# Feed-forward part of a hybrid decoder layer: one gate/up unit of the next group moved ahead of a group's down units, groups of 3, 4 and 4 slabs, transposes queued ahead of weight splits

## The chip, the cores and the metric

The kernel runs on one core of a Trainium2 chip. The metric is the device time of one execution in microseconds (us). The core has a matrix engine (TensorE, PE in the rows, with its weight loader PEld), a vector engine (VectorE, DVE), a scalar engine (ScalarE, ACT), GpSimd (POOL) and a queue engine (SyncE, SP), which here only issues DMAs. Each of them works through its own queue of instructions in order and waits on semaphores of the others.

## What is computed

One decoder layer on 256 tokens of width 2048: two attention mixers, merged and added to the input, and then a gated feed-forward part of width 5632. The change touches the last part alone:

```
hn = _rms(x, norm_ffn)                       # x: 256 x 2048, fp32
x = x + (silu(hn @ w_ffn_gate) * (hn @ w_ffn_up)) @ w_ffn_down
```

w_ffn_gate and w_ffn_up are 2048 x 5632, w_ffn_down is 5632 x 2048, all fp32 and read from HBM once.

## The kernel before, in words

**Precision.** Each product is made of three matmuls in the reduced fp32r format: an operand is split into hi (rounded, `L1059` for weights, on ACT) and lo (the rest, `L1060`, on DVE), and PE adds hi*hi, hi*lo and lo*hi (`L1084` to `L1086`) in PSUM.

**Steps and units.** The feed-forward part is a list of steps, objects of class `Pair`. A step takes two 128-row blocks of a weight (1 MB, two DMAs on SP into one of three `raw8` buffers). A plain step is 24 matmuls of 512 columns. A seven step (`mm_seven`) forms its 2x2 block product from seven instead of eight products and so needs 21 matmuls, but it has more to split: the weight is split in two parts, the second of sums that DVE forms first (`sums`, `L1051` to `L1054`). Four parts can be ahead of PE, since there are four hi/lo buffers; the sums have one.

A unit is 8 steps (or 6) that accumulate into the same PSUM banks. A gate/up unit of slab f makes 512 columns of the gated hidden activation from all of hn: steps 0, 2 and 4 are seven steps, except in slab 0, where all are plain. After the last seven step, `combine` adds the four banks of the seven-products on DVE (`L1121` to `L1124`; in the last group also the rows of the result so far, fetched by `fetch`, `L1127` to `L1130`); after the last step, `last` adds the rest (`L1141`) and `swiglu` forms the hidden slab (ACT `L1176`, DVE `L1180`) in two of the five `q2` buffers.

**Transposes.** A slab is the stationary operand of the down product, so it is transposed in two pairs by `hid_pair`: four PE transposes each (`L976`) into a PSUM bank of the kind that the seven-products use, then either `put_plain` (ACT copy `L950`, DVE difference `L951`, tile `ip`) or, for a pair that a seven step will use, `put_seven` (ACT `L958`, DVE `L962` to `L965`, ACT `L968`, DVE `L969`, tiles `F` and `i`). They hang on a step as hooks: (j, 0) before the step's matmuls, (j, 1) in the middle of them.

**Groups.** 11 slabs in groups of 4, 4 and 3. After the gate/up units of a group come its two down units (columns 0 to 1023 and 1024 to 2047 of the result), each with two steps for each slab: steps 0, 2 and 4 of 8, or 0 and 2 of 6, are seven steps. The first two groups add their result into `hacc` in HBM by accumulating DMAs on POOL; the last reads it back (`fetch`) and writes the output. Slab f is transposed in the unit that follows its gate/up unit, at the step after that unit's last seven step: step 5 of 8, step 3 of 6. For the last slab of a group this unit is the group's first down unit, whose last two steps use that slab.

**Order of instructions.** The loop at the end of the kernel goes through the steps and queues for each, in this order: `run_ffn(i)` (loads, and the splits of the parts that are now in reach), the hook (j, 0), the matmuls with the hook (j, 1) in their middle, then `combine` or `last`. On ACT and DVE the splits queued at a step thus stand ahead of its transposes.

In the text, "unit d0.0" is the first down unit of group 0, "g3" the gate/up unit of slab 3, and steps are counted from 0.

Of the kernel before, what the change touches and what calls it, by code (L numbers as in the profile page):

```python
# [14 lines left out]
P = 128  # L15
# [38 lines left out]
def hybrid_block(ctx: ExitStack, tc: tile.TileContext, x, norm_attn, w_in, fox_f_bias,  # L54
# [37 lines left out]
    def wk(shape, tag, bufs, dt=F32):  # L92
        pool = keep if tag in ("qs", "sm") else work
        return pool.tile(shape, dt, tag=tag, name=nm(tag), bufs=bufs)
# [8 lines left out]
    def load_x(q):  # L103
        for t in range(NT):
            nc.sync.dma_start(xin[t][:, q * 512:(q + 1) * 512], x[t * P:(t + 1) * P, q * 512:(q + 1) * 512])
# [7 lines left out]
    def load_vectors():  # L113
        nc.sync.dma_start(vec[16:32, :], norm_ffn.rearrange("(k p) -> k p", p=P))
        row = lambda a: a.rearrange("(o p) -> o p", o=1)
        nc.sync.dma_start(vec[32:33, :], row(fox_q_gain))
        nc.sync.dma_start(vec[33:34, :], row(fox_k_gain))
        for j, g in enumerate((nsa_q_gain, nsa_kc_gain, nsa_ks_gain, nsa_kw_gain)):
            nc.sync.dma_start(vec[34 + j:35 + j, :], row(g[0:P]))
            for o in (0, DK - P):  # L120
                nc.sync.dma_start(vec[38 + j:39 + j, o:o + DK - P], row(g[P:DK]))
        nc.sync.dma_start(pek, cmp_pe_k.rearrange("(j i) d -> j (i d)", i=2))
        nc.sync.dma_start(pev, cmp_pe_v)
        nc.sync.dma_start(fbias, fox_f_bias.partition_broadcast(P))
# [15 lines left out]
    def finish(tk):  # L140
        while not tk.over:
            tk.step()
        if tk in tasks:
            tasks.remove(tk)
# [12 lines left out]
    def load(ch):  # L157
        ch.raw = wpool.tile([P, 1024], F32, tag="raw", name=nm("raw"), bufs=RAW_BUFS)
        eng = nc.scalar if ch is stream[0] else nc.sync
        eng.dma_start(ch.raw[:, :ch.nkb * ch.n].rearrange("p (k n) -> p k n", k=ch.nkb),  # L160
                      ch.src.rearrange("(k p) n -> p k n", p=P))
        if ch is stream[0]:
            warm = wk([P, 16], "sm", 11)
            nc.scalar.activation(warm[:, 0:1], ident[:, 0:1], AF.Exp)
# [755 lines left out]
    def open2():  # L920
        left.close()
        pools[2] = left.enter_context(tc.tile_pool(name="pool2", bufs=1, reuse_waits="tile"))
# [5 lines left out]
    def p2(shape, tag, bufs, dt=F32):  # L928
        return pools[2].tile(shape, dt, tag=tag, name=nm(tag), bufs=bufs)
# [6 lines left out]
    SH = (0, 2, 4)  # L936
# [34 lines left out]
    def transpose_pair(make, srcs, c, seven, gains=None, where="tp"):  # L971

        b = bank(where)
        for k in range(2):
            for o, t in enumerate((1, 0) if seven and k == 0 else (0, 1)):
                nc.tensor.transpose(b[:, (2 * k + o) * P:(2 * k + o + 1) * P],  # L976
                                    srcs[t][:, c + k * P:c + (k + 1) * P], ident)
        dst = make(seven)
        (put_seven if seven else put_plain)(dst, b, gains)
        return dst  # L980

    hT = [None] * 8
    htask = {}
# [173 lines left out]

    hid = {}
    hsrc = {}
    GROUPS = ((0, 4), (4, 8), (8, 11))  # L1160
    SD = {8: (0, 2, 4), 6: (0, 2)}

    def make_hid(seven):
# [2 lines left out]
    def hid_pair(f, a, g):  # L1166
        f0, f1 = GROUPS[g]
        hid[f, a] = transpose_pair(make_hid, hsrc[f], a * 256, (f - f0) * 2 + a in SD[2 * (f1 - f0)],
                                   where="acc")

    def swiglu(f):
        def done(c, in_psum):
            g = {}
            for t in range(NT):
                g[t] = wk([P, 512], "qs", 4) if in_psum else c[t, 0]
                nc.scalar.activation(g[t], c[t, 0], AF.Silu, scale=rh[:, t:t + 1])  # L1176
            hsrc[f] = []
            for t in range(NT):
                o = p2([P, 512], "q2", 5) if in_psum else c[t, 1]
                nc.vector.scalar_tensor_tensor(o, c[t, 1], rh[:, t:t + 1], g[t], op0=ALU.mult, op1=ALU.mult)  # L1180
                hsrc[f].append(o)
        return done

    def two(w, r0, c0):
        return lambda kp: [w[r0 + kp * 2 * P:r0 + (kp + 1) * 2 * P, c:c + 512] for c in (c0, c0 + 512)]

    def down(g, i):
        pre = {}
        final = g == len(GROUPS) - 1
        cols = lambda c: slice((2 * i + c) * 512, (2 * i + c + 1) * 512)  # L1190

        def fetch():
            for t in range(NT):
                for c in range(2):
                    pre[t, c] = p2([P, 512], "q2", 5) if c else wk([P, 512], "qs", 4)
                    nc.gpsimd.dma_start(pre[t, c], hacc[t * P:(t + 1) * P, cols(c)])

        def done(c, in_psum):
            for t, h in ((0, 0), (1, 0), (0, 1), (1, 1)):
                rows = slice(t * P, (t + 1) * P)  # L1200
                if final:
                    nc.sync.dma_start(out[rows, cols(h)], c[t, h])
                else:
                    nc.gpsimd.dma_start(hacc[rows, cols(h)], c[t, h], accum_op=ALU.add)
        return fetch, done, (lambda: pre) if final else None

    pend = []

    def transposes(j):

        if not pend or j is None:
            return {}
        q = pend.pop()
        return {(j + 1, o): lambda o=o: hid_pair(q, o, g_of[q]) for o in range(2)}

    for g, (f0, f1) in enumerate(GROUPS):
        for f in range(f0, f1):
            sevens = SH if f else ()
            order = list(range(8))
            unit(order, sevens, lambda kp, f=f: [w[kp * 2 * P:(kp + 1) * 2 * P, f * 512:(f + 1) * 512]  # L1220
                                                 for w in (w_ffn_gate, w_ffn_up)],
                 lambda kp: hT[kp], swiglu(f), lambda kp: [htask[kp // 2]], transposes(max(sevens) if sevens else None))
            pend.append(f)
        n = 2 * (f1 - f0)
        order = list(range(n))
        for i in range(2):
            fetch, done, add = down(g, i)
            hooks = transposes(max(SD[n]))
            if add:
                hooks[0, 0] = fetch  # L1230
            unit(order, SD[n], two(w_ffn_down, f0 * 512, i * 1024),
                 lambda kp, f0=f0: hid[f0 + kp // 2, kp % 2], done, None, hooks, add)
    g_of = {f: g for g, (f0, f1) in enumerate(GROUPS) for f in range(f0, f1)}


    nload = nsplit = 0
    ffn = next(j for j, ch in enumerate(stream) if isinstance(ch, Pair))

    def split_ahead(i):
        return min(i + min(SPLIT_AHEAD, 2 + i // 4), ffn - 1)  # L1240

    def split_next():
        nonlocal nsplit
        split(stream[nsplit])
        nsplit += 1
        if nsplit == 1:
            transpose_gain(xT[0], xin, 0, VA)

    def run_att(i, ch):
        nonlocal nload  # L1250
        if i == n_att:
            open2()
        while nload < min(i + LOAD_AHEAD, ffn):
            if nload - nsplit >= RAW_BUFS:
                if nsplit <= split_ahead(i):
                    split_next()
                    continue
                break
            if nload < 8 and nload % 2 == 0:
                load_x(nload // 2)  # L1260
            load(stream[nload])
            nload += 1
            if nload == 9:
                load_vectors()
        while nsplit <= split_ahead(i):
            split_next()
# [28 lines left out]
    for i, ch in enumerate(stream):  # L1295
        if i < ffn:
            run_att(i, ch)
        if i + 8 >= ffn:
            run_ffn(i)
        if ch.need:  # L1300
            for tk in ch.need():
                finish(tk)
        if ch.pre:
            ch.pre()
        ch.mm(ch)
        if i in (0, 2, 4):
            transpose_gain(xT[i // 2 + 1], xin, i // 2 + 1, VA)
        if ch.done:
            ch.done()
        if i >= ffn:  # L1310
            ch.free()
            slot()
            slot()
            continue
        ch.raw = ch.hi = ch.lo = None
        if ch.nkb < 4:
            slot()
# [32 lines left out]
```

## Time and profile before

| | us |
|---|---|
| median of 3 runs (1457.8 to 1458.56) | 1458.3 |
| profiled execution, its own time | 1459.65 |
| span in that execution, first to last instruction | 1457.9 |
| feed-forward part in it, from 735.6 | 722 |

| engine | busy us | share of the span |
|---|---|---|
| PE | 1438.0 | 99% |
| PEld | 1206.2 | 83% |
| DVE | 1093.8 | 75% |
| ACT | 746.2 | 51% |
| POOL | 56.4 | 4% |

The profile is one execution, recorded by the hardware profiler. Times are counted from the first instruction. A row of the timeline gives start, duration, engine, line of the kernel, operation, output and inputs; a bracket at its end gives how long the engine had been idle before it and whose result ended that. A matmul of 512 columns is shown with 0.39 us, though the next one starts after 0.227 us: they overlap, and their ends are modelled. So one reads PE by starts, not by durations.

### The profile page before, as it was taken

The numbers are of one execution on the slowest core, as the hardware profiler recorded it, in microseconds if no ns is written. First come the engines' busy times: TensorE is split into PE (matmuls) and PEld (weight loads), VectorE is DVE, ScalarE is ACT, GpSimd is POOL, SyncE is SP. The second block draws the span as 40 slices with busy tenths as digits, with TensorE's granted clock in tenths as the row PEclk, the third lists the DMA queues.
The fourth block names the chain that finished last, engine by engine and source line by source line (L and its number), as shares of the span: only waits on it lengthen the run. The fifth ranks groups of instructions, "written<-read, shape, count | busy, mean of one in ns | idle before, by whom it ended". The sixth has DMA issues, their size and how long they took to land.

```text
span 1457.9 us, 18092 instructions
## 1 busy us (share of the span) xinstructions
PE 1438.0 (99%) x6772; PEld 1206.2 (83%) x6772; DVE 1093.8 (75%) x1408; ACT 746.2 (51%) x937; POOL 56.4 (4%) x75
## 2 busy tenths in 40 slices
PE   9999999999999999999999999999999999999978
PEld 7888888998888888888888888788888878888867
DVE  7766766776776555555666999878999997889976
ACT  6466554455666344445644455444554554445532
POOL 2001010000000000000000000000000000000000
PEclk9999999999999999999999999999999999999989
DMA  7576876457444666656764556678655667866653
GB/s 276 173 231 199 267 236 185 126 166 210 145 131 151 203 188 184 187 184 221 242 225 165 182 194 218 215 202 222 200 185 202 202 220 190 226 202 206 227 174 116
DMA packets 155395, 287.06 MB, mean 197 GB/s; under 512 B 9598, under 2 KB 32220, under 8 KB 155180
## 3 DMA queue, kind: packets, MB, share of 16 engines
q1 hardware_dynamic: 151260, 275.87, 59.9%
q0 software_dynamic: 3872, 9.78, 3.2%
q8 instruction: 53, 0.87, 0.2%
q10 hardware_dynamic: 176, 0.27, 0.1%
q14 instruction: 34, 0.28, 0.1%
HBM read 277.48 MB, written 8.40 MB: 196 GB/s over the span
## 4 chain that ended last, share of the span: by engine, by line
PE 96%; DVE 2%; issue 1%; ACT 0%; DMA 0%; POOL 0%; ACTq 0%; POOLq 0%; DVEq 0%
PE acc L193 14%; PE acc L194 14%; PE acc L195 14%; PE m L1086 12%; PE m L1084 12%; PE m L1085 12%; PE acc L1085 4%; PE acc L1084 4%; PE acc L1086 4%; PE m L536 1%; DVE lo L1060 1%; PE m L537 1%; PE acc L976 1%; DMA raw<-in_w_in_dram 0%; PE m L372 0%
## 5 line engine op out<-in xcount | busy, mean ns | idle before, releaser
L171 DVE TENSOR_TENSOR lo<-raw,hi 128x1024 fp32r<-128x1024 f32 (+5 forms) x261 | 306.4, 1179 | 169.8 <-ACT hi L170 169.2
L193 PE MATMUL acc<-hi,u 128*128 128x512 f32 (+4 forms) x960 | 374.8, 390 | 0.2 <-ACT u L270 0.2
L194 PE MATMUL acc<-lo,u 128*128 128x512 f32 (+4 forms) x960 | 368.3, 384 | 0.4 <-DVE lo L171 0.4
L195 PE MATMUL acc<-hi,u 128*128 128x512 f32 (+4 forms) x960 | 368.3, 384 | 0.0
L170 ACT ACTIVATE hi<-raw 128x1024 fp32r<-128x1024 f32 (+5 forms) x261 | 262.8, 1022 | 179.0 <-PE acc L195 166.3
L1060 DVE TENSOR_TENSOR lo<-raw,hi 128x2048 fp32r<-128x2048 f32 (+1 forms) x132 | 276.9, 2100 | 49.9 <-ACT hi L1059 49.8
L1059 ACT ACTIVATE hi<-raw 128x2048 fp32r<-128x2048 f32 (+1 forms) x132 | 231.9, 1762 | 142.7 <-PE m L1086 99.5
L195 PEld LDWEIGHTS acc<-hi,u 128*128 128x128 f32 x960 | 180.7, 188 | 33.1 <-DVE u L271 0.2
L193 PEld LDWEIGHTS acc<-hi,u 128*128 128x128 f32 x960 | 180.9, 188 | 30.7 <-ACT u L270 0.5
L194 PEld LDWEIGHTS acc<-lo,u 128*128 128x128 f32 x960 | 181.0, 189 | 30.2 <-DVE lo L171 1.0
L1084 PE MATMUL m<-hi,hp 128*128 128x512 f32 x400 | 157.4, 393 | 0.0
L1086 PE MATMUL m<-hi,hp 128*128 128x512 f32 x400 | 156.2, 390 | 0.0
L1085 PE MATMUL m<-lo,hp 128*128 128x512 f32 x400 | 155.9, 390 | 0.0
L1059 ACT ACTIVATE hi<-sums 128x2048 fp32r<-128x2048 f32 x46 | 88.2, 1917 | 126.2 <-DVE sums L1054 83.8
L1060 DVE TENSOR_TENSOR lo<-sums,hi 128x2048 fp32r<-128x2048 f32 x46 | 105.4, 2292 | 32.6 <-ACT hi L1059 32.6
L1086 PE MATMUL m<-hi,ip 128*128 128x512 f32 x224 | 90.1, 402 | 12.4 <-DVE ip L951 12.4
L1084 PE MATMUL m<-hi,ip 128*128 128x512 f32 x224 | 89.9, 401 | 0.0
L1085 PE MATMUL m<-lo,ip 128*128 128x512 f32 x224 | 89.4, 399 | 0.0
L1086 PEld LDWEIGHTS m<-hi,hp 128*128 128x128 f32 x400 | 75.1, 188 | 15.8
L1085 PEld LDWEIGHTS m<-lo,hp 128*128 128x128 f32 x400 | 75.2, 188 | 15.2
L1084 PEld LDWEIGHTS m<-hi,hp 128*128 128x128 f32 x400 | 75.2, 188 | 15.1
L1086 PEld LDWEIGHTS m<-hi,ip 128*128 128x128 f32 x224 | 43.5, 194 | 23.0 <-DVE ip L951 13.7
(300 smaller groups left out, 1791.2 us busy)
## 6 DMA issues: line engine op xcount, KB each, us to landing
raw<-in_w_in_dram SPq DMA_DIRECT2D x127, 512.0 KB
raw<-in_w_ffn_gate_dram SPq DMA_DIRECT2D x88, 512.0 KB
raw<-in_w_ffn_up_dram SPq DMA_DIRECT2D x88, 512.0 KB
raw<-in_w_ffn_down_dram SPq DMA_DIRECT2D x88, 512.0 KB
raw<-in_w_out_dram SPq DMA_DIRECT2D x32, 512.0 KB
raw<-in_w_in_dram SPq DMA_DIRECT2D x24, 384.0 KB
raw<-in_w_up_fox_dram SPq DMA_DIRECT2D x16, 512.0 KB
raw<-in_w_up_nsa_dram SPq DMA_DIRECT2D x16, 512.0 KB
```

The source lines that it names most:

```text
L170: nc.scalar.activation(hi[:, :m], ch.raw[:, :m], AF.Copy)
L171: nc.vector.tensor_tensor(lo[:, :m], ch.raw[:, :m], hi[:, :m].bitcast(F32), op=ALU.subtract)
L193: nc.tensor.matmul(o, h, ch.hi[:, j], start=first and j == 0, stop=False)
L194: nc.tensor.matmul(o, h, ch.lo[:, j], start=False, stop=False)
L195: nc.tensor.matmul(o, l, ch.hi[:, j], start=False, stop=last and j == w - 1)
L536: nc.tensor.matmul(o, s, ch.hi[:, j], start=j == 0, stop=False)
L537: nc.tensor.matmul(o, s, ch.lo[:, j], start=False, stop=j == 3)
L1059: nc.scalar.activation(h, src, AF.Copy)
L1060: nc.vector.tensor_tensor(l, src, h.bitcast(F32), op=ALU.subtract)
L1084: nc.tensor.matmul(o, h, hi, start=n == 0, stop=False)
L1085: nc.tensor.matmul(o, h, lo, start=False, stop=False)
L1086: nc.tensor.matmul(o, l, hi, start=False, stop=n + 1 == total[key])
```

## The change

The groups become 3, 4 and 4 slabs. The gate/up unit of the next group's first slab is put ahead of a group's two down units, so that the last slab of the first two groups is transposed in that gate/up unit (step 5), and that next slab itself in the group's second down unit (step 3 of 6 or 5 of 8). In the last group, where no slab follows, the first down unit takes its steps in the order 0, 1, 2, 4, 3, 5, 6, 7, so that its three seven steps are the places 0, 2 and 3, and the last slab is transposed at place 4. And in the loop the hook (j, 0) of a feed-forward step is called ahead of `run_ffn(i)`, so that its transposes, and the loads of `fetch`, are queued before that step's loads and weight splits; the hook (j, 1) stays where it was.

```
--- before.py
+++ after.py
@@ -1157,7 +1157,7 @@
 
     hid = {}
     hsrc = {}
-    GROUPS = ((0, 4), (4, 8), (8, 11))
+    GROUPS = ((0, 3), (3, 7), (7, 11))
     SD = {8: (0, 2, 4), 6: (0, 2)}
 
     def make_hid(seven):
@@ -1204,33 +1204,39 @@
                     nc.gpsimd.dma_start(hacc[rows, cols(h)], c[t, h], accum_op=ALU.add)
         return fetch, done, (lambda: pre) if final else None
 
-    pend = []
-
-    def transposes(j):
-
-        if not pend or j is None:
-            return {}
-        q = pend.pop()
-        return {(j + 1, o): lambda o=o: hid_pair(q, o, g_of[q]) for o in range(2)}
-
+    def transposes(f, j):
+
+        return {(j, o): lambda o=o: hid_pair(f, o, g_of[f]) for o in range(2)}
+
+    def gate_up(f, hooks):
+        sevens = SH if f else ()
+        unit(list(range(8)), sevens, lambda kp: [w[kp * 2 * P:(kp + 1) * 2 * P, f * 512:(f + 1) * 512]
+                                                 for w in (w_ffn_gate, w_ffn_up)],
+             lambda kp: hT[kp], swiglu(f), lambda kp: [htask[kp // 2]], hooks)
+
+    def down_unit(g, i, order, hooks):
+        f0, f1 = GROUPS[g]
+        fetch, done, add = down(g, i)
+        if add:
+            hooks = {**hooks, (0, 0): fetch}
+        unit(order, SD[2 * (f1 - f0)], two(w_ffn_down, f0 * 512, i * 1024),
+             lambda kp: hid[f0 + kp // 2, kp % 2], done, None, hooks, add)
+
+    g_of = {f: g for g, (f0, f1) in enumerate(GROUPS) for f in range(f0, f1)}
+    at = {8: 5, 6: 3}
     for g, (f0, f1) in enumerate(GROUPS):
-        for f in range(f0, f1):
-            sevens = SH if f else ()
-            order = list(range(8))
-            unit(order, sevens, lambda kp, f=f: [w[kp * 2 * P:(kp + 1) * 2 * P, f * 512:(f + 1) * 512]
-                                                 for w in (w_ffn_gate, w_ffn_up)],
-                 lambda kp: hT[kp], swiglu(f), lambda kp: [htask[kp // 2]], transposes(max(sevens) if sevens else None))
-            pend.append(f)
         n = 2 * (f1 - f0)
         order = list(range(n))
-        for i in range(2):
-            fetch, done, add = down(g, i)
-            hooks = transposes(max(SD[n]))
-            if add:
-                hooks[0, 0] = fetch
-            unit(order, SD[n], two(w_ffn_down, f0 * 512, i * 1024),
-                 lambda kp, f0=f0: hid[f0 + kp // 2, kp % 2], done, None, hooks, add)
-    g_of = {f: g for g, (f0, f1) in enumerate(GROUPS) for f in range(f0, f1)}
+        more = g + 1 < len(GROUPS)
+
+        for f in range(f0 + (1 if g else 0), f1 + (1 if more else 0)):
+            gate_up(f, transposes(f - 1, 5) if f > f0 + (1 if g else 0) else {})
+        if more:
+            down_unit(g, 0, order, {})
+            down_unit(g, 1, order, transposes(f1, at[n]))
+        else:
+            down_unit(g, 0, [0, 1, 2, 4, 3, 5, 6, 7], transposes(f1 - 1, 4))
+            down_unit(g, 1, order, {})
 
 
     nload = nsplit = 0
@@ -1295,12 +1301,14 @@
     for i, ch in enumerate(stream):
         if i < ffn:
             run_att(i, ch)
+        if i >= ffn and ch.pre:
+            ch.pre()
         if i + 8 >= ffn:
             run_ffn(i)
         if ch.need:
             for tk in ch.need():
                 finish(tk)
-        if ch.pre:
+        if i < ffn and ch.pre:
             ch.pre()
         ch.mm(ch)
         if i in (0, 2, 4):
```

## Rows read from the trace of the kernel before

**Rows 1.** The page, first part: busy time, share of the span, instructions.

```profile
PE 1438.0 (99%) x6772; PEld 1206.2 (83%) x6772; DVE 1093.8 (75%) x1408; ACT 746.2 (51%) x937; POOL 56.4 (4%) x75
```

**Rows 2.** Waits of PE and PEld: total us, times, longest us.

```profile
PE m L1086 <- DVE ip L951: 12.4, 3, 7.5
...
PEld acc L1085 <- DVE lo L1060: 1.9, 8, 0.5
```

**Rows 3.** Timeline, PE: first matmuls of steps of d0.0 and d0.1, d1.0, d2.0.

```profile
939.25 0.39 PE L1084 MATMUL m<-hi,ip 128*128 128x512 f32 x1
...
949.09 0.39 PE L1084 MATMUL m<-hi,ip 128*128 128x512 f32 x1
...
954.53 0.39 PE L1084 MATMUL acc<-hi,i 128*128 128x512 f32 x1
...
1196.97 0.39 PE L1084 MATMUL m<-hi,ip 128*128 128x512 f32 x1
...
1206.57 0.39 PE L1084 MATMUL m<-hi,ip 128*128 128x512 f32 x1
...
1401.41 0.39 PE L1084 MATMUL m<-hi,ip 128*128 128x512 f32 x1
...
1417.07 0.39 PE L1084 MATMUL m<-hi,ip 128*128 128x512 f32 x1
```

**Rows 4.** Timeline, PE: the three matmuls that waited for a transposed slab.

```profile
942.33 0.50 PE L1086 MATMUL m<-hi,ip 128*128 128x512 f32 x1 [2.47 <-DVE ip L951]
...
1200.05 0.80 PE L1086 MATMUL m<-hi,ip 128*128 128x512 f32 x1 [2.46 <-DVE ip L951]
...
1409.54 0.80 PE L1086 MATMUL m<-hi,ip 128*128 128x512 f32 x1 [7.52 <-DVE ip L951]
```

**Rows 5.** Stages: us, each engine's busy time, granted clock, DMA share, GB/s.

```profile
960.00:1000.00 40.00, 40.00 (x178) 33.15 (x177) 34.12 (x29) 18.94 (x12) 3.46 (x4) 1.00 0.81 234
1000.00:1150.00 150.00, 149.96 (x671) 123.71 (x670) 135.16 (x117) 80.28 (x56) 0.00 (x0) 1.00 0.65 204
1395.00:1425.00 30.00, 22.48 (x92) 18.14 (x91) 20.86 (x23) 9.69 (x7) 2.16 (x4) 0.83 0.59 187
```

**Rows 6.** Timeline, DVE and one row of ACT: step 5 of g3; step 2 of d0.0.

```profile
892.59 2.28 DVE L1060 TENSOR_TENSOR lo<-raw,hi 128x2048 fp32r<-128x2048 f32 x1
894.79 1.22 DVE L1051 TENSOR_TENSOR sums<-raw 128x1024 f32<-128x1024 f32 x1
...
897.38 1.75 DVE L1060 TENSOR_TENSOR lo<-raw,hi 128x1536 fp32r<-128x1536 f32 x1
899.05 0.29 DVE L962 TENSOR_TENSOR F<-F 128x128 f32<-128x128 f32 x1
...
901.14 1.09 DVE L969 TENSOR_TENSOR i<-F,i 128x896 fp32r<-128x896 f32 x1 [1.08 <-ACT i L968]
901.50 1.91 ACT L1059 ACTIVATE hi<-sums 128x2048 fp32r<-128x2048 f32 x1
902.15 0.68 DVE L951 TENSOR_TENSOR ip<-acc,ip 128x512 fp32r<-128x512 f32 x1
903.44 2.29 DVE L1060 TENSOR_TENSOR lo<-sums,hi 128x2048 fp32r<-128x2048 f32 x1 [0.60 <-ACT hi L1059]
...
916.28 2.29 DVE L1060 TENSOR_TENSOR lo<-sums,hi 128x2048 fp32r<-128x2048 f32 x1 [0.38 <-ACT hi L1059]
```

**Rows 7.** Timeline, PEld and DVE: step 2 and step 5 of d0.0.

```profile
918.63 0.19 PEld L1085 LDWEIGHTS acc<-lo,i 128*128 128x128 f32 x1 [0.20 <-DVE lo L1060]
...
941.59 1.28 DVE L951 TENSOR_TENSOR ip<-acc,ip 128x512 fp32r<-128x512 f32 x2
```

**Rows 8.** Timeline of d2.0: PE's step 2, and DVE around it.

```profile
1390.15 0.39 PE L1084 MATMUL acc<-hi,i 128*128 128x512 f32 x1
...
1390.87 4.49 DVE L1060 TENSOR_TENSOR lo<-raw,hi 128x2048 fp32r<-128x2048 f32 x2
...
1398.73 0.69 DVE L1123 TENSOR_TENSOR q<-acc,qs 128x512 f32<-128x512 f32 x1 [2.04 <-PE acc L976]
```

## The prediction

> **What bounds the kernel.** I read the first part of the page first [rows 1]: PE is busy 99% of the span, the other engines far less. So only time in which PE stands or runs slowly can be won, unless it gets less work, and it does not: the diff only reorders. In groups of 4, 4 and 3 the down units have 2 x (3 + 3 + 2) = 16 seven steps, in 3, 4 and 4 just as many; matmuls, transposes, splits, loads and the accumulating DMAs keep their number. Next I read the waits of PE [rows 2]: of all its waits in the feed-forward part, one matters, 12.4 us in 3 waits for the DVE half of a transposed slab (L951). The timeline places them [rows 4]: 2.47, 2.46 and 7.52 us, in the first down unit of each group, where the unit's last steps use the slab that was only just made.
>
> The wait is not all that is lost. The step beginning at 939.25 ends at 949.09 and takes 9.84 us; the next, also 24 matmuls, ends at 954.53 and takes 5.44 us [rows 3]. The stages show why [rows 5]: the granted clock, 1.00 between 960 and 1150 us, is 0.83 in the stage of the longest wait, so after it matmuls run for a while at 1.2 instead of 2.4 GHz. Reading the reader should take along: a step's length from start to start holds both losses.
>
> Why is the slab late? DVE. At step 5 its queue holds a split, sums and a second split ahead of the transposes' DVE work: in the like step of g3 that is 892.59 to 899.05, 6.5 us [rows 6]; in d0.0 L951 comes only at 941.59, 2.3 us after PE wanted it at the step begun at 939.25 [rows 3, 7]. And DVE has little room: 135.16 of 150 us busy [rows 5].
>
> **What the change removes.** Three long steps, each against 5.44 us: 9.84 - 5.44 = 4.40; 1206.57 - 1196.97 = 9.60, so 4.16; 1417.07 - 1401.41 = 15.66, so 10.22 [rows 3]. Sum 18.78 us. Will they go wholly? In groups 0 and 1 the last slab is now transposed in the next gate/up unit, at its step 5; three more steps of 5.4 us and four or six steps of the down unit lie before its use, some 37 us against a lateness of 2.5. In the last group the transposes move to place 4 and their uses are at places 6 and 7. Behind the fourth step's end DVE does four combine operations and four adds of 0.7 us, and may stand 2.04 us for a buffer that the transposes free, as in the old d2.0 [rows 8]: 7.7 us at most until the first pair's L951 can start, since no split stands ahead of it any more. Place 6 begins 5.4 + 6.0 us after place 4. The second pair lies behind two splits of 2.28 us [rows 6]: 13 us, against 17 at place 7. Cover of some 3.5 us each; I take the whole 18.78. What is late next is DVE's weight splits, which come now.
>
> **What it adds, first: two seven steps in a row (d2.0, places 2 and 3).** In the old d2.0 step 2 begins at 1390.15 and the DVE work for its second part ends at 1390.87, where the next split starts [rows 8], just in time. Now a seven step's splits must follow: sums 2.59 us (894.79 to 897.38), first split 1.75, 0.38 waiting for ACT's hi of the sums, second split 2.29 [rows 6], less 0.1 where they overlap: ready at 1390.87 + 6.9 = 1397.8. PE would want it 21 matmuls and four more after 1390.15; at 5.44/24 = 0.227 us each that is 1395.8. So PE waits 2.0 us. Whether the clock then falls no row of such a wait shows. The nearest are the waits of 2.47 and 2.46 us, whose steps lost 1.93 and 1.70 us beyond the wait [rows 3, 4]; the other side is PEld's waits of up to 0.5 us with next to none [rows 2]. 2.0 is nearer to 2.46, so I take 1.8 us. Together 3.8, bounds 2.0 and 4.0; a gain is excluded, as the work on DVE does not shrink.
>
> **Second: the new queue order.** The first pair's transposes now stand ahead of two splits. Their PE part starts when the preceding step ends, and so do the hi splits, which wait for the buffers of that step, so little is held back; but a seven pair bounces DVE, ACT, DVE. In g3 DVE stands 1.08 us for L968, and later 0.60 us for the hi of the sums [rows 6]. With the pair in front, the 1.08 stays; then lo of the next split (2.28) must wait for its hi, which ACT can start only after L968: the hi takes 1.91 us, and L969 covers 1.09 of it, so some 0.9 us are new; the 0.60 goes, since sums and ACT have run on by then. Net 0.2 to 0.3 us later on DVE. This lands on the tightest place there is: the second part of the next unit's step 2, for which PEld already waits 8 times, 1.9 us in all [rows 2], once at 918.63 for 0.20 us [rows 7] behind the split at 916.28 [rows 6]. A later DVE goes straight to PE there. Before, eight units lie behind a gate/up unit with a seven pair; now six do, as two of those pairs are made in down units, which have no swiglu work. 6 x 0.3 = 1.8 more, less the two places that vanish and some overlap of PEld: I take 1.0 us. Bounds: nothing, if ACT's hi fits under L969, and 6 x 0.9 = 5.4, if the 0.60 does not come back. A gain is excluded, since the same work on DVE gets one more wait.
>
> **Free of cost.** Loads: SP's queue has the same transfers, a gate/up unit's ahead of a down unit's, one for one. POOL: sixteen accumulating DMAs as before; `fetch` is queued a moment earlier on POOL, which is idle 96% of the time [rows 1]. The first slab of the next group holds two of five q2 buffers through d0.0 and d0.1, so the second combine there makes a sixth claim. Nearest row: 2.04 us on DVE [rows 8]; the down units have room for it, so 0, at worst 2 x 2.
>
> **Sum.** -18.78 + 3.8 + 1.0 = -14.0 us. The profiled execution took 1459.65 us, so it would take 1445.7; it stands 1.35 above the median of 1458.3, so the forecast for the median is 1444.3 us.
>
> The Trainium skill would price the loss otherwise: "Perfetto Trace Analysis", section "Identifying the Most-Contended Engine", holds matmul busy time a poor measure and weight-load busy time a good one. From 1395 to 1425 the loads are busy 18.14 us; undisturbed they are 33.15 in 40, or 83%, so 18.14 stands for 21.9 us of work and 8.1 lost, where the steps say 10.2 [rows 5]. Scaled to all three that is 14.9 in place of 18.78 and a time near 1448. I stay with the steps, since a load at the lower clock counts as busy too.
>
> **The rivals.**
> - *The clock falls anyway*: the slow stretches are not the waits' doing and only the 12.45 us of waits go [rows 4]; 1458.3 - 12.45 + 4.8 = 1450.7. Against it, the clock is 1.00 in the 190 us between two waits [rows 5]. Chance 0.04.
> - *DVE gives it back in part*: each of the six places loses 0.9 instead of 0.2, and the buffers cost 4: 1458.3 - 18.78 + 3.8 + 5.4 + 2 = 1450.7 or a little more. For it, DVE at 90% with a wait already at that place [rows 2, 5]; against, 0.60 us of slack per unit. Chance 0.11.
> - *The change doesn't do what it says in the last group*: the slab is late there still, behind combine, adds and the buffer; 10.22 stays and only the other two go: 1458.3 - 8.56 + 4.8 = 1454.5. Against, 3.5 us of cover. Chance 0.06.
> - *Slower*: DVE becomes the bound. At the step 2 behind every unit with a transposed seven pair (eight) PE would wait so long that the clock falls, 2.0 + 1.8 us as in d2.0: 8 x 3.8 = 30.4; 1458.3 - 18.78 + 3.8 + 30.4 = 1473.7. It decides from 15 / 8 = 1.9 us of loss at each place, seven times what I work out. Chance 0.03.
>
> **How the numbers follow.** Forecast 0.76: within 1441 (no clock fall, nothing for the queue order) and 1447. The range adds the first two rivals in part, down to 1440.5 and up to 1450.5, which leaves out the last two and half of the others, some 0.17. A measurement of this kernel tells about 0.2%, 2.9 us, from no change. Faster by more than that: the forecast, the first three rivals less a little, 0.94; within it 0.03; slower 0.03.
>
> **What would show it.** Right: no wait of PE for L951; the three clock dips replaced by at most one, in d2.0; one wait of PE of about 2 us for a split there at place 3; step 2 behind the six units 0.2 to 0.3 us longer; L962 ahead of the first split of its step on DVE. Wrong: PE waits for splits above 0.5 us in gate/up units (second rival), a long step at places 6 or 7 of d2.0 (third), clock dips without a wait (first).

## The result, and the profile after

The changed kernel takes 1442.7 us (median of 5 runs, 1442.43 to 1445.15), the kernel before in the same runs 1457.8 (1457.18 to 1458.56): a ratio of 0.9901, 95% interval 0.9886 to 0.9915, faster by 15.1 us. The forecast was 1444.3 us, in a range of 1440.5 to 1450.5. The profiled execution took 1442.43 us with a span of 1440.7.

The page of the changed kernel, busy times and granted clock in 40 slices of the span. Beside [rows 1], PE is busy 6.1 us less with the same 6772 instructions. 5.4 us of that lie in the feed-forward part, where the matmuls at 1.2 GHz were. The clock (PEclk, in tenths of full speed, 9 for 90% or more) stands at 9 in every slice.

```profile
PE 1431.9 (99%) x6772; PEld 1201.3 (83%) x6772; DVE 1093.6 (76%) x1408; ACT 745.5 (52%) x937; POOL 56.1 (4%) x75
...
PEclk9999999999999999999999999999999999999999
```

The waits of PE and PEld of the changed kernel, which answer to [rows 2]. The row of PE for L951 is gone; in its place stands one wait for a split. PEld again has eight waits for splits, but not in the same places: six of 0.32 to 0.33 us, at step 2 behind six gate/up units, and two at place 3 of d2.0, of 0.41 and 2.1 us. (Place k is the k-th step that a unit does, counted from 0; in d2.0 that is no longer step k.)

```profile
PE acc L1085 <- DVE lo L1060: 1.7, 1, 1.7
...
PEld acc L1085 <- DVE lo L1060: 4.5, 8, 2.1
```

The timeline of PE in d2.0 of the changed kernel: place 3 (from 1365.32), place 4 (from 1372.72) and the first matmuls of places 5 to 7. Place 6, the first that uses the last slab, takes 5.44 us; the first such step of the old d2.0 took 15.66 [rows 3]. What is lost stands at place 3: 7.40 us to the next step, of which 0.36 are the transposes ahead of that, where an undisturbed seven step has 4.76; the loss is 2.28 us.

```profile
1365.32 0.39 PE L1084 MATMUL acc<-hi,i 128*128 128x512 f32 x1
...
1368.38 0.50 PE L1085 MATMUL acc<-lo,i 128*128 128x512 f32 x1 [1.72 <-DVE lo L1060]
...
1372.72 0.48 PE L1084 MATMUL m<-hi,ip 128*128 128x512 f32 x1
...
1378.78 0.39 PE L1084 MATMUL m<-hi,ip 128*128 128x512 f32 x1
...
1384.22 0.39 PE L1084 MATMUL m<-hi,ip 128*128 128x512 f32 x1
...
1389.66 0.39 PE L1084 MATMUL m<-hi,ip 128*128 128x512 f32 x1
```

To keep noise of the attention part out, the experiments below are also compared by a length read from the timeline of one profile each: from the first feed-forward matmul to the start of the last step. The first matmul's start varies between 734.6 and 736.4 us from one profile to the next, whatever the kernel. The length repeats better: the two profiles of the changed kernel in the table differ by 0.02 us. Of the kernel before there is only one profile, an execution of 1459.65 us, 1.85 above the median here.

| kernel | median of its runs (lowest to highest), us | feed-forward length, us |
|---|---|---|
| before | 1457.8 (1457.18 to 1458.56) | 712.73 |
| changed | 1442.7 (1442.43 to 1445.15) | 696.57 |
| queue order alone | 1444.42 (1444.11 to 1444.72) | 697.67 |
| regrouping alone | 1443.41 (1442.78 to 1443.48) | 696.22 |
| d2.0 in natural order | 1443.76 (1443.25 to 1444.14) | 697.29 |
| seven steps first in d2.0 | 1451.07 (1450.54 to 1451.46) | 704.42 |
| changed, second set | 1444.15 (1442.82 to 1445.16) | 696.55 |
| regrouping alone, second set | 1443.52 (1442.85 to 1443.79) | 696.11 |
| two seven steps in d2.0 | 1441.59 (1441.43 to 1442.26) | 694.99 |
| the same, old queue order | 1441.03 (1440.87 to 1441.61) | 694.25 |

### The profile page after: what moved, and what is told of

It is laid out like the page before. It is cut to its first block, busy times and chain, and to the rows that moved or that the text cites. A ratio compares the mean times of both kernels' runs of the same rounds, so it can differ in the third digit from the quotient of the medians.

```text
span 1440.7 us, 18109 instructions
## 1 busy us (share of the span) xinstructions
PE 1431.9 (99%) x6772; PEld 1201.3 (83%) x6772; DVE 1093.6 (76%) x1408; ACT 745.5 (52%) x937; POOL 56.1 (4%) x75
## 4 chain that ended last, share of the span: by engine, by line
PE 96%; DVE 2%; ACT 1%; issue 1%; DMA 0%; POOL 0%; SPq 0%; ACTq 0%; POOLq 0%; DVEq 0%
PE acc L193 15%; PE acc L194 15%; PE acc L195 14%; PE m L1086 11%; PE m L1084 11%; PE m L1085 11%; PE acc L1085 4%; PE acc L1086 4%; PE acc L1084 4%; DVE lo L1060 1%; PE m L536 1%; PE m L537 1%; PE acc L976 1%; ACT hi L1059 1%; DMA u<-in_x_dram 0%
## 5 line engine op out<-in xcount | busy, mean ns | idle before, releaser
L1084 PEld LDWEIGHTS m<-hi,hp 128*128 128x128 f32 x400 | 75.1, 188 | 15.1
L1084 PE MATMUL m<-hi,ip 128*128 128x512 f32 x224 | 87.7, 392 | 0.0
L1086 PE MATMUL m<-hi,ip 128*128 128x512 f32 x224 | 87.3, 390 | 0.0
L1085 PE MATMUL acc<-lo,h 128*128 128x512 f32 x144 | 56.6, 393 | 0.0
```

Of the source, the lines that this page charges most:

```text
L1084: nc.tensor.matmul(o, h, hi, start=n == 0, stop=False)
L1085: nc.tensor.matmul(o, h, lo, start=False, stop=False)
L1086: nc.tensor.matmul(o, l, hi, start=False, stop=n + 1 == total[key])
```

## The experiments

**The queue order alone.** The loop's edit on the kernel before, nothing else:

```
+        if i >= ffn and ch.pre:
+            ch.pre()
         if i + 8 >= ffn:
             run_ffn(i)
...
-        if ch.pre:
+        if i < ffn and ch.pre:
             ch.pre()
```

> The kernel before with the queue order alone: groups of 4, 4 and 3 and the order of units stay, the hook ahead of a step's matmuls is called before that step's loads and splits. Theory A (the slab was late because splits stood ahead of its transposes on DVE): the first pair is now ahead of them; the second pair still stands behind 6.5 us of splits, but is wanted a step later. So the waits in d0.0 and d1.0 go wholly, and in d2.0, where combine, its buffer wait and the adds come first, two waits of about 1.6 us each stay instead of one of 7.5. Gain 8.6 + 7.0, less about 1 us that the queue order costs at the eight places with a seven pair: some 14.6 us, 1443 to 1444.5 us. Theory B (the regrouping is what wins, the queue order only supports it): a gain under 5 us, above 1453 us.

Measured: ratio 0.9907 (0.9892 to 0.9922), 13.5 us off the median of 1457.89 in the same set, and 15.06 us off the feed-forward length. PE's timeline in the old d2.0, three steps from their first matmuls: the steps that were 15.66 and 5.44 us long take 6.81 and 7.06, with a short wait in each (1.6 us each were expected); d0.0 and d1.0 have no wait for L951 left.

```profile
1393.41 0.39 PE L1084 MATMUL m<-hi,ip 128*128 128x512 f32 x1
...
1395.08 0.50 PE L1086 MATMUL m<-hi,ip 128*128 128x512 f32 x1 [1.06 <-DVE ip L951]
...
1400.22 0.39 PE L1084 MATMUL m<-hi,ip 128*128 128x512 f32 x1
...
1402.13 0.50 PE L1086 MATMUL m<-hi,ip 128*128 128x512 f32 x1 [1.30 <-DVE ip L951]
...
1407.28 0.39 PE L1084 MATMUL acc<-hi,i 128*128 128x512 f32 x1
```

Theory A holds, and with it the cause: the slab was late because its DVE work stood behind splits. One call moved ahead brings most of the gain. The second wait is still the second pair, which the hook in the step's middle leaves behind the splits. DVE of this kernel:

```profile
1394.35 0.68 DVE L951 TENSOR_TENSOR ip<-acc,ip 128x512 fp32r<-128x512 f32 x1
1394.95 2.28 DVE L1060 TENSOR_TENSOR lo<-raw,hi 128x2048 fp32r<-128x2048 f32 x1
...
1401.40 0.68 DVE L951 TENSOR_TENSOR ip<-acc,ip 128x512 fp32r<-128x512 f32 x1
```

The moved call changes ACT's queue as well. That ACT was not what made the slab late shows in the kernel before: in its d2.0 the copies of both pairs on ACT (L950) ran from 1400.41 to 1401.47, and DVE came to its half only 7.3 us later, without a pause between 1398.73 and then. In d0.0 too the copies were done, at 938.4, before L951 began at 941.59.

```profile
1400.41 1.06 ACT L950 ACTIVATE ip<-acc 128x512 fp32r<-128x512 f32 x2
...
1408.80 1.28 DVE L951 TENSOR_TENSOR ip<-acc,ip 128x512 fp32r<-128x512 f32 x2
```

**The regrouping alone.** The changed kernel with the old order of hook and `run_ffn`:

```
-        if i >= ffn and ch.pre:
-            ch.pre()
         if i + 8 >= ffn:
             run_ffn(i)
...
-        if i < ffn and ch.pre:
+        if ch.pre:
             ch.pre()
```

> The changed kernel with the loop of the kernel before: the hook ahead of a step's matmuls is called after that step's loads and splits again. Theory A: in groups 0 and 1 the slab has units of time, so no wait there; in d2.0 the first pair now stands behind two splits as well, ready 12.2 us after place 4 begins where place 6 wants it after 11.5, a wait of 0 to 1 us. Step 2 behind the six units with a seven pair in a gate/up unit takes 4.85 us instead of 4.97. In all within 1 us of the changed kernel, 1441.7 to 1443.5 us. Theory B (the queue order is needed): a wait for the transposed slab of 3 us or more at place 6 of d2.0, 1446 us or more.

> The regrouping without the queue order, once more, beside the changed kernel. Theory A (from the steps of the two profiles: it wins 6 x 0.12 us at the six step 2 and loses 0.33 us at place 6 and 0.07 at place 3 of d2.0): 0.3 us faster than the changed kernel, which the times can hardly tell. Theory B (the medians of the two separate sets mean something): 0.7 us slower.

Measured: ratio 0.9899 (0.9882 to 0.9915), and in the second set 0.9902 (0.9888 to 0.9917) beside 0.9910 (0.9893 to 0.9926) for the changed kernel. The feed-forward lengths say 0.35 and 0.44 us less than the changed kernel, as expected 0.3; the times can't tell the two apart. The timeline shows both sides of it: the seven step 2 of g10, 4.84 us from start to start here, and 4.97 in the changed kernel (1317.68 to 1322.65 in the fence after it); against that PEld waits for the slab in d2.0, where place 6 takes 5.77 us.

```profile
1318.51 0.39 PE L1084 MATMUL acc<-hi,h 128*128 128x512 f32 x1
...
1323.35 0.39 PE L1084 MATMUL m<-hi,hp 128*128 128x512 f32 x1
...
1385.48 0.19 PEld L1086 LDWEIGHTS m<-hi,ip 128*128 128x128 f32 x1 [0.45 <-DVE ip L951]
```

PE of the changed kernel, the same step:

```profile
1317.68 0.39 PE L1084 MATMUL acc<-hi,h 128*128 128x512 f32 x1
...
1322.65 0.39 PE L1084 MATMUL m<-hi,hp 128*128 128x512 f32 x1
```

So either half of the change alone removes nearly all of the old waits (the queue order leaves 1.06 and 1.30 us in d2.0, the regrouping 0.45 us of PEld), and the two do not add up.

**d2.0 in natural order.**

```
-            down_unit(g, 0, [0, 1, 2, 4, 3, 5, 6, 7], transposes(f1 - 1, 4))
+            down_unit(g, 0, order, transposes(f1 - 1, 5))
```

> The changed kernel with d2.0's steps in their natural order, 0 to 7, and the last slab transposed at step 5. Theory A: the 2.28 us at the two seven steps in a row go, but the first pair is wanted one step after its transposes and stands behind combine, a buffer wait and the adds (a wait of some 1.6 us), and the second behind two splits and sums besides (another 1.7 us). About 1 us slower than the changed kernel, 1443 to 1445 us. Rival: these are hidden, and the kernel gains the 2.3 us, 1440.4 us.

Measured: ratio 0.9902 (0.9887 to 0.9917), a feed-forward length 0.72 us above the changed kernel. Its waits of PE have one line for the slab, for the two places 6 and 7:

```profile
PE m L1086 <- DVE ip L951: 2.4, 2, 1.3
```

Places 6 and 7 lose 1.36 and 1.62 us as steps. The reordered d2.0 trades this for the 2.28 us at its place 3 and wins a little; theory A.

**Seven steps first in d2.0.**

```
-            down_unit(g, 0, [0, 1, 2, 4, 3, 5, 6, 7], transposes(f1 - 1, 4))
+            down_unit(g, 0, [0, 2, 4, 1, 3, 5, 6, 7], transposes(f1 - 1, 4))
```

> The changed kernel with d2.0's steps in the order 0, 2, 4, 1, 3, 5, 6, 7, so that all three seven steps come first: a look at the price of seven steps in a row, and at the clock. Theory A (each seven step behind a seven step needs 6.9 us of DVE where PE has 4.8): PE waits about 1.1 and 2.0 us in place 1 and 2.0 us in place 2, 5.1 us in place of 2.5. If no wait of about 2 us lets the clock fall: 1445.3 us, granted clock 1.00 throughout. If waits that come so near to each other do: 1.8 us or more on top, 1447 to 1449 us, and matmuls at 1.2 GHz after them.

Measured: 1451.07 us, beyond both numbers. Places 0 to 2 lose 0.70, 2.56 and 2.29 us, 5.5 in all where 5.1 was expected, with waits of 1.83 and 1.70 us and no fall of the clock behind them. But place 5 takes 10.24 us instead of 5.44, which I had not foreseen. PE's timeline of this kernel, places 1 and 2 and then place 5 with its slow matmuls:

```profile
1359.20 0.50 PE L1085 MATMUL acc<-lo,i 128*128 128x512 f32 x1 [1.83 <-DVE lo L1060]
...
1366.24 0.50 PE L1085 MATMUL acc<-lo,i 128*128 128x512 f32 x1 [1.70 <-DVE lo L1060]
...
1382.08 0.39 PE L1084 MATMUL m<-hi,ip 128*128 128x512 f32 x1
...
1385.36 0.67 PE L1085 MATMUL m<-lo,ip 128*128 128x512 f32 x1 [2.89 <-DVE lo L1060]
1385.82 0.63 PE L1086 MATMUL m<-hi,ip 128*128 128x512 f32 x1
...
1392.32 0.39 PE L1084 MATMUL m<-hi,ip 128*128 128x512 f32 x1
```

DVE's timeline says why: combine now comes after place 2, but its third operation needs a q2 buffer that the transposes of place 4 free, and it stands 7.49 us for them, with the splits for place 5 (from 1383.02) behind it.

```profile
1371.23 0.69 DVE L1122 TENSOR_TENSOR qs<-acc,q 128x512 f32<-128x512 f32 x1
1379.41 0.69 DVE L1123 TENSOR_TENSOR q<-acc,qs 128x512 f32<-128x512 f32 x1 [7.49 <-PE acc L976]
...
1383.02 4.48 DVE L1060 TENSOR_TENSOR lo<-raw,hi 128x2048 fp32r<-128x2048 f32 x2
```

It is the wait of 2.04 us of [rows 8], grown because the transposes are one step further behind combine. The changed kernel has it as well, at 2.04 us, since there the transposes follow combine at once.

**Two seven steps in d2.0.** The pair that was the third seven step gets a tile with eight slots instead of seven, which a plain step can read too; d2.1 still uses it as a seven step. The last argument of `down_unit`, new here, names the steps of this unit that are seven steps.

```
+    def make_hid8(seven):
+        return p3([P, 2, 8, P], "i7", 3, F32R)
...
-        hid[f, a] = transpose_pair(make_hid, hsrc[f], ...
+        hid[f, a] = transpose_pair(make_hid8 if (f, a) == (9, 0) else make_hid, hsrc[f], ...
...
-            down_unit(g, 0, [0, 1, 2, 4, 3, 5, 6, 7], transposes(f1 - 1, 4))
+            down_unit(g, 0, order, transposes(f1 - 1, 3), (0, 2))
```

> The changed kernel once more, as the measure for the three others of this set: 1442.5 to 1443 us. Its steps: step 2 behind six gate/up units takes 4.97 us (0.21 over an undisturbed seven step), place 3 of d2.0 takes 7.40 with the transposes behind it (2.28 us over).

> The changed kernel with two seven steps instead of three in d2.0, in natural order, and the last slab transposed at step 3; the pair that was the third seven step is kept in a tile that serves a plain step there and a seven step in d2.1. Theory A (the wait at place 3 is DVE's splits of two seven steps in a row): three matmuls more, 0.68 us, and 2.28 us less waiting, step 4 plain and undisturbed at 5.44: 1.6 us faster than the changed kernel, about 1441.1 us. Rival: DVE's lag only moves, PE waits for splits or the slab later in d2.0, and the time is that of the changed kernel or more.

> As two_sevens, and with the loop of the kernel before (the hook ahead of a step's matmuls after that step's splits). The last slab now has three steps between its transposes and its use, so it needs no place ahead of the splits. Theory A: the six step 2 go back to 4.85 us, 0.7 us faster than two_sevens and 2.3 us faster than the changed kernel, about 1440.4 us. Rival: the slab is late at step 6 of d2.0, and nothing is won over two_sevens.

Measured: 1441.59 and 1441.03 us, 0.5 and 0.6 above what was expected, beside 1444.15 for the changed kernel, which lies above its own 1442.5 to 1443 (see below). All runs of both lie below the lowest of the changed kernel in this set, 1442.82. The lengths are 1.56 and 2.30 us shorter than the changed kernel's, as expected 1.6 and 2.3. PE and PEld of the second one have no wait above 0.4 us left in the feed-forward part; PEld's row for splits reads:

```profile
PEld acc L1085 <- DVE lo L1060: 1.3, 6, 0.3
```

So three matmuls more are cheaper than the wait, and with the slab's transposes three steps ahead of its use the queue order buys nothing and costs 0.74 us.

**Does the clock fall at place 3?** The second set of the changed kernel lies higher, and single runs of it, at 1444.57 and 1445.16 us, have a mean granted clock of 0.998 and 0.997. The mean alone does not say where the clock fell: the last kernel above, with no such wait, has 0.998 in its profile too, and there the clock is 0.97 in the first 50 us and 1.00 in the feed-forward part. Three more profiles of the changed kernel:

> The changed kernel, one more profile. Open: the two wait profiles show no clock below 1.00 in the feed-forward part, but some timed executions (1444.6 to 1445.2 us) have a mean granted clock of 0.997 or 0.998. Theory A: the wait of 1.7 us at place 3 of d2.0 lets the clock fall in some executions; such a profile has matmuls at 1.2 GHz behind it and a time 1.5 to 2.5 us above 1442.5. Theory B: those executions lose it at the kernel's start, and place 3 takes 7.4 us in each.

> As after_look1: the same kernel, another execution. Theory A: 1.5 to 2.5 us more where the clock falls at d2.0. Theory B: place 3 of d2.0 takes 7.4 us whatever the time.

> As after_look1: the same kernel, another execution. Theory A: 1.5 to 2.5 us more where the clock falls at d2.0. Theory B: place 3 of d2.0 takes 7.4 us whatever the time.

Measured: 1444.09, 1445.71 and 1445.73 us. In the first the feed-forward length is 696.62, in the other two 698.36 and 698.30. The stage around place 3, with each engine's busy time and then the granted clock, in the second of the three:

```profile
1365.00:1377.00 12.00, 10.28 (x39) 7.71 (x38) 10.29 (x7) 6.71 (x6) 0.00 (x0) 0.86 0.56 182
```

and in the changed kernel's first profile:

```profile
1364.00:1376.00 12.00, 10.28 (x49) 7.89 (x47) 9.63 (x6) 8.40 (x6) 0.00 (x0) 1.00 0.62 202
```

PE's timeline of that second one has the same wait, 1.72 us, but place 3 lasts from 1367.00 to 1376.00, 9.00 us in place of 7.40 to 7.48. Behind the wait some matmuls start 0.43 us apart instead of 0.227:

```profile
1367.00 0.39 PE L1084 MATMUL acc<-hi,i 128*128 128x512 f32 x1
...
1370.05 0.50 PE L1085 MATMUL acc<-lo,i 128*128 128x512 f32 x1 [1.72 <-DVE lo L1060]
...
1372.32 0.63 PE L1085 MATMUL acc<-lo,i 128*128 128x512 f32 x1
1372.75 0.63 PE L1086 MATMUL acc<-hi,i 128*128 128x512 f32 x1
...
1376.00 0.48 PE L1084 MATMUL m<-hi,ip 128*128 128x512 f32 x1
```

Theory A: the same kernel with the same wait (1.70 to 1.73 us) meets a fall of the clock in two of five profiles, and it costs 1.6 us at place 3. In the two profiles of the regrouping alone, which have this wait too, the clock does not fall. The first of the three, 1444.09 us, has no fall; its time is longer by as much as its feed-forward part starts late (736.18 instead of 734.57). So about as much again of the spread comes from ahead of the feed-forward part, where theory B looked. But it is not the clock there, as theory B had it: the mean clock of that profile is 1.000. What moves that start stays open.

## Why the prediction was right, step by step

- *What is removed*: right. The feed-forward length falls by 16.16 us; with the 2.28 us at place 3 and a net 0.3 at the six places (below) that makes 18.7 us of waits and slow matmuls gone, the 18.78 of the sum. Both figures take the kernel before from the same trace, so they agree on one thing only: that nothing of the three long steps stayed. Counting step lengths rather than waits was what made this term right: the waits alone were 12.45 us. The reading by weight-load busy time, after the Trainium skill ("Perfetto Trace Analysis", section "Identifying the Most-Contended Engine"), gave 14.9 us, 4 us short. That section of the Trainium skill names the share of weight-load busy time as a measure of how close a kernel is to roofline. Scaling it to a loss was my own step, and for a loss that is partly a lower clock the measurement decides against it. In the slow stretches of the kernel before, a load took 0.33 us instead of 0.19, and so counted as more work than it was:

```profile
944.41 0.33 PEld L1085 LDWEIGHTS m<-lo,ip 128*128 128x128 f32 x1
```

- *Two seven steps in a row*: place and cause were right. PE stood 1.72 us where 2.0 was worked out, since it had already waited at place 2 and at place 3's beginning; as a step it lost 2.28.
- *The clock behind it*: this is the term that failed. I took 1.8 us from the nearest rows, the waits of 2.46 us. It was nothing in three of five profiles and 1.6 us in two. Wait and clock together were priced at 3.8 us where the profile without a fall shows 2.28. Against the 16.16 us of the feed-forward length the sum's 14.0 is 2.2 too small: 1.5 of that is here, 0.7 the queue order. That the forecast is only 1.6 us above the median is in part luck: the medians fell by 15.1 us, a us less than the length, which rests on the one, rather slow profiled execution of the kernel before. Had I split this term by chance, the sum would have been nearer to the length.
- *The queue order*: right in kind, too large by 0.7. Each of the six places takes 4.97 or 4.98 us: 0.21 us over an undisturbed seven step, 0.13 more than in the regrouping alone, where I had 0.3 before the overlap of PEld. As worked out, DVE waits 1.08 us for L968 as before and then for the hi of the next split, 0.71 instead of 0.9, and the 0.60 of [rows 6] is gone. DVE of the changed kernel, g10's step 5:

```profile
1337.24 1.09 DVE L969 TENSOR_TENSOR i<-F,i 128x896 fp32r<-128x896 f32 x1 [1.08 <-ACT i L968]
1339.05 2.29 DVE L1060 TENSOR_TENSOR lo<-raw,hi 128x2048 fp32r<-128x2048 f32 x1 [0.71 <-ACT hi L1059]
```

- *Cover in the last group*: right. In the changed kernel the first pair's L951 starts at 1379.71, 7.0 us into place 4 (7.7 were allowed), and the second's at 1384.72, 12.0 us in (13 allowed); places 6 and 7 begin at 1384.22 and 1389.66:

```profile
1379.71 0.68 DVE L951 TENSOR_TENSOR ip<-acc,ip 128x512 fp32r<-128x512 f32 x1
1380.32 4.48 DVE L1060 TENSOR_TENSOR lo<-raw,hi 128x2048 fp32r<-128x2048 f32 x2
1384.72 0.68 DVE L951 TENSOR_TENSOR ip<-acc,ip 128x512 fp32r<-128x512 f32 x1
```

- *The buffers*: nothing in the changed kernel, as taken. But the bound of 2 us each was too small as a bound: the wait that it was taken from grew to 7.49 us in another order of steps.
- *The rivals*: the clock does fall without the old waits, but only behind the new one. DVE gives back 0.3 us net, not 5. (That rival's sum adds 2 us for the buffers where its text says 4; with 4 it is 1452.7.) Nothing is late at places 6 and 7. The slower case did not come near: it needed 1.9 us at each of eight places.

What the prediction did not see: that the two halves of the change do nearly the same thing. The queue order by itself takes 15.06 of the 16.16 us; I costed it only as a loss, because in the changed kernel it is one.

## What to carry to other kernels

When an engine waits for a small piece of work on a busy in-order engine, look first at what is queued ahead of it there: moving a call ahead of the splits did nearly what a new order of units did. Beside a wait, measure the whole step from start to start, since the slow clock behind a wait can cost nearly as much as the wait (1.9 us behind one of 2.47). And when the work of two engines per step is uneven, do not put the steps that are heavy for the hidden engine next to each other; a little more work on the bound engine (0.68 us here) can be cheaper than the wait (2.28 us).

## What the runs showed of the hardware

The clock's fall behind a wait is not a matter of the wait's length alone. The waits of 7.52, 2.47, 2.46 and 2.89 us were each followed by matmuls at 1.2 GHz; the waits of 1.83, 1.30 and 1.06 us were not; one and the same wait of 1.70 to 1.73 us was followed by it in two of five profiles of one kernel and cost 1.6 us there. What decides between the two cases no run here shows. A wait of this size is better priced with a chance than with a yes or no.
